# Cross attention's query projection with the tokens' high and low part moving together, and another order of the first loads

## The chip, the cores and the metric

The kernel is one layer of a decoder and runs on one core of a Trainium2 chip. The metric is the time of one execution on the device in microseconds (us), taken as the median of several runs. The engines of the core are named as in the profile: PE is TensorE's matmul and PEld its weight load, DVE is VectorE, ACT is ScalarE, POOL is GpSimd, SP is SyncE, which here only issues transfers.

## The reference

All of it is float32, with 256 tokens of width 1024 (`x`), 256 memory tokens (`mem`) and one layer:

```python
z = h @ w_in[l]                                  # u | q | k | v, 512 columns each
pool_out = multiscale_pool(u, w_pool[l], pool_scale[l])
attn_out = moba_attention(q, k, v)               # 8 heads of 64; at 256 tokens plain causal attention
mix = jnp.concatenate([pool_out, attn_out], axis=-1) @ w_out[l]
h = layer_norm(DEEPNORM_ALPHA * h + mix, ln1_g[l], ln1_b[l])
h = layer_norm(DEEPNORM_ALPHA * h + memory_cross_attention(h, mem, w_xq[l], w_xkv[l], w_xo[l]),
               ln2_g[l], ln2_b[l])
h = layer_norm(DEEPNORM_ALPHA * h + swiglu(h, w_gate[l], w_up[l], w_down[l]), ln3_g[l], ln3_b[l])

def memory_cross_attention(h, mem, w_xq, w_xkv, w_xo):   # 4 heads of 256
    q = (h @ w_xq).reshape(B_, S_, XATTN_HEADS, XATTN_HEAD_DIM)
    kv = mem @ w_xkv
    ...
    s = jnp.einsum('bshd,bmhd->bhsm', q, k, ...) * (XATTN_HEAD_DIM ** -0.5)
    p = jax.nn.softmax(s, axis=-1)
    o = jnp.einsum('bhsm,bmhd->bshd', p.astype(v.dtype), v).reshape(B_, S_, D)
    return o @ w_xo
```

`swiglu` has 2816 hidden columns: `(silu(h @ w_gate) * (h @ w_up)) @ w_down`.

## The kernel before

**Products in three parts.** Each operand of a large product is split into a high part, which is the number rounded to `float32r`, and a low part, which is what is left. A product is then high by high, high by low and low by high, three matmuls that add up in PSUM. `split` does this for activations: ScalarE copies the high part (line 319), VectorE subtracts it (line 320). `split_scaled` (lines 323 and 324) does the same with a factor. `Both` keeps a high and a low part side by side in one tile, so that one matmul can move both, 512 columns wide.

**The stream of weights.** `Stream` (`ws`) holds all weights as numbered tiles in the order of their use: w0 to w14 for queries, keys and values (w0 to w5 are 128 x 512, the next 128 x 1024), then the pooling input, cross attention's keys, the output projection, cross attention's values (w35 to w42), cross attention's queries (`c_xq`, w43 to w50, two tiles of four rows of k for each head), its output projection (w51 to w58), the gate and up weights (`c_gu`, from w59, four tiles for each of eleven chunks) and the down projection. `fetch` issues the transfers, seven raw tiles ahead. `prepare` casts a tile to its high part on ScalarE (line 95) and subtracts it on VectorE into the low part (line 96). There are eight high and eight low buffers, so tile i goes into the place of tile i - 8. `get` hands out a tile, and on the way prepares one more tile if fewer than `used + 8` are prepared; `done` counts `used` up when the last row of a tile has been multiplied. The order of the instructions on every engine is the order in which the code emits them: the schedule is written by hand, with generators that `run` advances by a given number of steps.

**The start.** `keep_busy` gives TensorE matmuls on zeros. The tokens come transposed, in blocks of 128 rows (`load_xt`, line 198): the first on SP's queue, the second on ScalarE's. Tile w0 comes in two halves by `ws.cuts`: the first on ScalarE's queue, the second on SP's. Then w1, w2, w3 and so on follow on SP's queue. `ws.casts` cuts the cast of w0 into three. `product_qk` (line 390) multiplies w0 with the first block of tokens, then w1 with the same block, then w2 and w3 with the second block.

**Cross attention.** `h1T` holds the tokens transposed, as two tiles, one for the high and one for the low part. `do_xq(h)` projects a head's queries with `proj_t` (line 274): for each of eight rows k and each of two halves f three matmuls of 256 columns, into one PSUM bank, then one `split_scaled` for the whole head. It yields 16 times. `xscores(h)` multiplies the queries with the keys (lines 256 to 258; the queries' parts are the stationary operand), takes maximum, exponentials and sum, and scales. `xprobs_t(h)` transposes the probabilities (line 716) and splits them, `xattend(h)` multiplies them with the values. The heads are interleaved by hand: five steps of head h + 1 stand between the projection of head h and its scores, up to head 2. The scores of head 3 come behind three steps of the output projection `project(c_xo, ...)`.

**Feed-forward.** `product_gu` makes a chunk's gate and up products in four PSUM banks: a pass over eight rows with the high weights, each moving both parts of `h2T` (line 804, 512 columns), then a pass with the low weights that moves the high part alone (line 811, 256 columns). In the first of these chunks `gated_t` (line 793) transposes the gated first chunk `sg0` in the middle of the high pass. `Gated.add` (lines 830 and 831) adds the two parts of a chunk.

Of the kernel before, what the change touches and what calls it, by code (L numbers as in the profile page):

```python
# [8 lines left out]
F32 = mybir.dt.float32  # L9
F32R = mybir.dt.float32r  # L10
AF = mybir.ActivationFunctionType
OP = mybir.AluOpType
AX = mybir.AxisListType

P = 128
D = 1024
S = 256
T = S // P
KD = D // P
# [12 lines left out]
RAW_BUFS, W_BUFS, AHEAD = 7, 8, 8  # L32
A8_BUFS = 9
PR_BUFS = 6
# [3 lines left out]
def r32(t):  # L38
    return t.bitcast(F32)


class Stream:
# [40 lines left out]
    def prepare(self, upto, eng=None):  # L83
        nc = self.nc
        while len(self.tiles) < min(upto, len(self.src)):
            i = len(self.tiles)
            src = self.src[i]
            for split in self.splits.pop(i, []):
                split()
            self.fetch(i + 1, nc.sync)  # L90
            raw = self.raws[i]
            hi = self.pool.tile(list(src.shape), F32R, tag="hi", name=f"w{i}h")
            lo = self.pool.tile(list(src.shape), F32R, tag="lo", name=f"w{i}l")
            for s in self.casts.get(i, [slice(None)]):
                nc.scalar.copy(hi[:, :, s], raw[:, :, s])  # L95
            (eng or nc.vector).tensor_sub(lo, raw, r32(hi))
            self.tiles.append((hi, lo))
            self.fetch(max(i + 1, len(self.homes)) + RAW_BUFS, nc.sync)

# [26 lines left out]
def decoder_layer(  # L126
# [3 lines left out]
    nc = tc.nc  # L130
# [3 lines left out]
    sp = ctx.enter_context(tc.tile_pool(name="small", bufs=3))  # L134
# [6 lines left out]
    def a8(name, dt=F32):  # L141
        return ap.tile([P, KD, S], dt, tag="a8", name=name)

    def bank(name):
        return pb.tile([P, 512], F32, tag="b", name=name)
# [5 lines left out]
    ws = Stream(nc, wp)  # L151

    def cols(w, c):

        return ws.add(w[c])
# [4 lines left out]
    def block(w, at, shape):  # L160

        j, n = shape
        return w[at:at + P * j * n].rearrange("(p j n) -> p j n", p=P, j=j)
# [6 lines left out]
        else:  # L170
            c_qk.append(ws.add(block(w_qkv, k * P * 1024, (2, 512)), 1))
    c_v = [ws.add(block(w_qkv, (KD + i) * P * 1024, (2, 512)), 1) for i in range(KD // 2)]
    ws.cuts[0] = [(slice(0, 256), nc.scalar), (slice(256, 512), nc.sync)]
    ws.casts[0] = [slice(0, 128), slice(128, 256), slice(256, 512)]
    c_u = [cols(w_u, c) for c in range(2)]
    c_xk = [cols(w_xk, c) for c in range(4)]
    c_mix = [rows(w_out, k, 0) for k in range(KD)]
# [1 line left out]
    c_xq = [cols(w_xq, c) for c in range(4)]  # L179
    c_xo = [rows(w_xo, k, 0) for k in range(KD)]  # L180
    c_gu = [ws.add(w_gu[c], 4) for c in range(NFC)]
# [10 lines left out]
    xr = a8("xr")  # L192
# [1 line left out]
    ws.homes = [home[0][:, n:n + 1, :] for n in range(4)]  # L194
    ws.homes += [home[1][:, 0:1, :], home[1][:, 1:2, :], home[1][:, 2:4, :]]

    def load_xt(k, n=2, queue=nc.sync):
        queue.dma_start(xr[:, k:k + n, :], block(x_t, k * P * S, (n, S)))

    def split_xt(k, n=2):  # L200
        split(xT[0][:, k:k + n, :], xT[1][:, k:k + n, :], xr[:, k:k + n, :])
# [58 lines left out]
    def pair(hl, *ix):  # L260
        return hl[0][ix], hl[1][ix]
# [3 lines left out]
    def proj_t(pss, numbers, yT):  # L265


        for k in range(KD):
            hi, lo = ws.get(numbers, k)
            y_hi, y_lo = pair(yT, ALL, k)  # L270
            for f in range(2):
                s = slice(f * P, (f + 1) * P)
                for n, (w, y) in enumerate(((hi, y_hi), (hi, y_lo), (lo, y_hi))):
                    nc.tensor.matmul(pss[f], w[:, s], y, start=k == 0 and f == 0 and n == 0,  # L274
                                     stop=k == KD - 1 and n == 2, skip_group_check=True)
                if f == 1:
                    ws.done(numbers, k)
                yield
# [31 lines left out]
    def run(gen, n=None):  # L310

        while n is None or n > 0:
            if next(gen, gen) is gen:
                return False
            n = None if n is None else n - 1
        return True

    def split(h, l, ps):
        nc.scalar.copy(h, ps)  # L319
        nc.vector.tensor_sub(l, ps, r32(h))  # L320

    def split_scaled(h, l, ps, scale):
        nc.scalar.mul(h, ps, scale)  # L323
        nc.vector.scalar_tensor_tensor(l, ps, scale, r32(h), op0=OP.mult, op1=OP.subtract)  # L324
# [18 lines left out]
    def transpose_tok(dst, tok, t, k0):  # L343

        ps = bank("tp")
        for k in range(4):
            nc.tensor.transpose(ps[:, k * P:(k + 1) * P], tok[:, (k0 + k) * P:(k0 + k + 1) * P], ident)  # L347
        ts = slice(t * P, (t + 1) * P)
        h, l = dst.parts(k0, 4, ts) if isinstance(dst, Both) else (d[:, k0:k0 + 4, ts] for d in dst)
        split(h, l, ps.rearrange("p (k t) -> p k t", k=4))  # L350


    qkT = a8("qkT")
# [11 lines left out]
    def keep_qk(i):  # L365

        dst = qkT[:, 2 * i:2 * i + 2, :]
        if i == 0:
            nc.scalar.mul(dst, qk[i], HD ** -0.5)
        elif i == 1:  # L370
            nc.vector.tensor_scalar(dst, qk[i], HD ** -0.5, None, op0=OP.mult)
        elif i == 2:
            nc.scalar.copy(dst, qk[i])
        else:
            nc.vector.tensor_copy(dst, qk[i])

    def product_qk(k):


        x_hi, x_lo = pair(xT, ALL, k)  # L380
        for j in range(2):
            hi, lo = ws.get(c_qk[k], j)
            halves = (2 * j, 2 * j + 1)
            order = [(i, f, hi, y) for i in halves for f in range(2) for y in (x_hi, x_lo)]
            if k == j == 0:
                order = [(i, f, hi, y) for i in halves for y in (x_hi, x_lo) for f in range(2)]
            order += [(i, f, lo, x_hi) for i in halves for f in range(2)]
            for i, f, w, y in order:
                c = 2 * (i % 2) + f
                nc.tensor.matmul(qk[i][:, f, :], w[:, c * P:(c + 1) * P], y,  # L390
                                 start=k == 0 and f == 0 and w is hi and y is x_hi,
                                 stop=k == KD - 1 and w is lo, skip_group_check=True)
                if k == KD - 1 and w is lo and f == 1:
                    keep_qk(i)
            ws.done(c_qk[k], j)
# [2 lines left out]
    for k in range(2, KD, 2):  # L398
        ws.before_split(c_qk[k][0], lambda k=k: split_xt(k))
    load_xt(0, 1)  # L400
    ws.fetch(1, None)
    load_xt(1, 1, nc.scalar)
    ws.fetch(4, nc.sync)
    load_xt(2)
    ws.fetch(7, nc.sync)
    load_xt(4)
# [263 lines left out]
        norm.finish()  # L670
    run(mix)
    ws.held = False
    h1T = (a8("h1Th", F32R), a8("h1Tl", F32R))

    xv = [ap.tile([P, T, D], F32R, tag="a8", name=f"xv{i}") for i in range(2)]

# [16 lines left out]
    oT = (a8("oTh", F32R), a8("oTl", F32R))  # L693
    xqT, xpr, xpt = {}, {}, {}

    def do_xq(h):
        ps = (bank if h == 0 else accbank)("pxq").rearrange("p (f t) -> p f t", f=2)
        yield from proj_t([ps[:, f, :] for f in range(2)], c_xq[h], h1T)
        xqT[h] = [sp.tile([P, 2, S], F32R, name=f"xq{i}", tag="pr", bufs=PR_BUFS) for i in range(2)]
        split_scaled(*xqT[h], ps, 256 ** -0.5)  # L700

    def xscores(h):
        ps = bank("xs").rearrange("p (t s) -> p t s", t=2)
# [25 lines left out]
    xq = [do_xq(h) for h in range(XH)]  # L729
# [3 lines left out]
    run(xq[1])  # L733
    run(xq[2], 5)
    xscores(1)
    run(xq[2], 6)
    xprobs_t(0)
    run(xq[2])
    run(xq[3], 6)
    xscores(2)  # L740
    xattend(0)
    run(xq[3], 6)
    xprobs_t(1)
    run(xq[3])

# [13 lines left out]
    h2T = Both("h2T")  # L759
# [29 lines left out]
    def gated_t():  # L789
        pt = bank("pgt").rearrange("p (f t) -> p f t", f=2)  # L790
        for t in range(T):
            for f in range(2):
                nc.tensor.transpose(pt[:, f, t * P:(t + 1) * P], sg0[:, t, f * P:(f + 1) * P], ident)
        split(gT[0][0][:, 0:2, :], gT[0][1][:, 0:2, :], pt)

    def product_gu(pss, numbers):

        n = ws.src[numbers[0]].shape[1]  # L800
        for k in range(KD):
            hi, _ = ws.get(numbers, k)
            for b, ps in enumerate(pss):
                nc.tensor.matmul(ps, hi[:, b * P:(b + 1) * P], h2T.both(k), start=k == 0, stop=False,  # L804
                                 skip_group_check=True)
            if k % n == n - 1:
                yield
        for k in range(KD):
            _, lo = ws.parts_of(numbers, k)
            for b, ps in enumerate(pss):  # L810
                nc.tensor.matmul(ps[:, S:], lo[:, b * P:(b + 1) * P], h2T.pair(k)[0], start=False,  # L811
                                 stop=k == KD - 1, skip_group_check=True)
            ws.done(numbers, k)
            if k % n == n - 1:
                ws.prepare(min(ws.used + AHEAD, len(ws.tiles) + 1))
                yield

    class Gated:


# [31 lines left out]
    left = None  # L852
    for c in range(1, NFC):
        pss = [(accbank if c % 2 else bank)("pg") for _ in range(4)]
        gu = product_gu(pss, c_gu[c])
        run(gu, 1)
        if left:
            left.multiply()
        run(gu, 1)
        if left:  # L860
            left.split()
        else:
            gated_t()
        run(gu)
        left = Gated(c, pss)
        left.add()
# [37 lines left out]
    left = until(dn)[1]  # L904
# [57 lines left out]
```

## Time and profile before

| | |
|---|---|
| median of 3 runs | 384.67 us (384.36 to 385.12) |
| profiled execution | 384.89 us, span 383.1 us from the first to the last instruction |
| granted TensorE clock, mean | 0.995 |
| TensorE busy | 373.4 us, 97% of the span |
| VectorE, ScalarE, GpSimd busy | 259.7, 187.6 and 19.0 us |
| the chain that ended last | 94% on TensorE |
| transfers | 71.93 MB, mean 188 GB/s |
| stretch of the query projections (131.78 to 163.33 us) | TensorE busy 31.55 us of 31.55, VectorE 21.42, ScalarE 15.72 |

The rows of a timeline begin with start and duration in us, then the engine, the line of the code, the operation, `out<-in` by the program's names and the shapes; in brackets stands how long the engine was idle before it and what ended that. Rows of matmuls can overlap, since they are pipelined: their starts are what counts. A row of the waits names who waited, on whom, and then the total in us, the number of times and the longest. `DMA` in the chain is a transfer, from its issue to its landing.

### The profile page before, as it was taken

The page shows a single profiled execution, that of the slowest core. Times are in us where ns is not written, and L with a number is a line of the kernel's source. Part 1 is how long each engine was busy: PE and PEld are TensorE (multiplying, and loading weights), DVE is VectorE, ACT ScalarE, POOL GpSimd, SP SyncE. Part 2 cuts the span into 40 slices and gives each one's busy share as a digit, 9 for nine tenths or more (in the row PEclk, how much of TensorE's full clock was granted, in tenths as well). Part 3 has the DMA queues.
Part 4 walks back from the last instruction along what each step waited for, and adds up shares of the span by engine and source line. Part 5 has one row for each costly group of instructions (what it writes and reads, how often), then busy time and mean ns, then how long its engine had stood idle before and what let it go on. Part 6 is the DMA issues. An engine that isn't in the chain of part 4 may idle for free.

```text
span 383.1 us, 5778 instructions
## 1 busy us (share of the span) xinstructions
PE 373.4 (97%) x2236; PEld 330.2 (86%) x2236; DVE 259.7 (68%) x390; ACT 187.6 (49%) x293; POOL 19.0 (5%) x31
## 2 busy tenths in 40 slices
PE   8999999999999999999999999999999999999992
PEld 7997989898888899988887888888888888888881
DVE  5758889954699766665888766666776667444275
ACT  5646677544164644454147455566445564334000
POOL 1000036300010000000100000000000000000000
PEclk9999999999999999999999999999999999999998
DMA  8997674668509953433109854456655758630011
GB/s 266 409 413 252 214 285 120 229 193 284 169 1 325 357 196 116 137 134 109 56 0 322 285 174 165 171 204 220 217 187 153 285 178 270 194 110 2 0 46 64
DMA packets 21322, 71.93 MB, mean 188 GB/s; under 512 B 2480, under 2 KB 3504, under 8 KB 21168
## 3 DMA queue, kind: packets, MB, share of 16 engines
q1 hardware_dynamic: 20720, 71.05, 54.2%
q10 hardware_dynamic: 576, 0.52, 0.4%
q8 instruction: 17, 0.28, 0.3%
q14 instruction: 9, 0.07, 0.0%
HBM read 70.52 MB, written 1.05 MB: 187 GB/s over the span
## 4 chain that ended last, share of the span: by engine, by line
PE 94%; ACT 1%; DVE 1%; DMA 1%; issue 1%; SPq 0%; DVEq 0%; ACTq 0%
PE pg L804 18%; PE pg L811 10%; PE acc L256 9%; PE acc L257 9%; PE acc L258 9%; PE pxq L274 6%; PE pxk L274 6%; PE pqk L390 6%; PE pu L274 3%; PE xv L258 2%; PE xv L256 2%; PE xv L257 2%; DMA wr<-in_w_qkv 1%; PE pv L256 1%; PE pv L257 1%; PE pv L258 1%
## 5 line engine op out<-in xcount | busy, mean ns | idle before, releaser
L830 ACT COPY sg<-pg 128x256 f32<-128x256 f32 x40 | 12.0, 387 | 23.5 <-PE pg L811 23.5
L611 POOL TENSOR_TENSOR rs<-rs,mhalf 128x1 f32<-128x1 f32 x6 | 5.0, 832 | 302.5 <-DVE rs L610 302.5
L835 ACT ACTIVATE sg<-sg 128x512 f32<-128x512 f32 x10 | 6.3, 633 | 16.7 <-DVE sg L831 16.7
L831 DVE TENSOR_TENSOR sg<-pg,sg 128x256 f32<-128x256 f32 x40 | 14.1, 414 | 0.0
L600 DVE SCALAR_TENSOR_TENSOR r<-h,acc 128x256 f32<-128x256 f32 (+1 forms) x10 | 5.1, 519 | 10.9 <-PE acc L258 10.9
L320 DVE TENSOR_TENSOR gTl<-sg,gTh 128x512 fp32r<-128x512 f32 x10 | 6.9, 692 | 6.2 <-ACT gTh L319 6.2
L426 ACT ACTIVATE pr<-pr,mx 128x128 f32<-128x128 f32 (+1 forms) x16 | 7.1, 445 | 6.8 <-DVE mx L457 6.8
L319 ACT CAST gTh<-sg 128x512 fp32r<-128x512 f32 x10 | 6.2, 621 | 7.8 <-DVE sg L836 7.8
L426 ACT ACTIVATE xpr<-xs,mx 128x256 f32<-128x256 f32 x8 | 3.7, 470 | 10.2 <-DVE mx L437 10.2
L319 ACT CAST h2T<-tp 128x512 fp32r<-128x512 f32 x4 | 2.4, 588 | 12.9 <-PE tp L347 12.9
L603 DVE BATCH_NORM_STATS2 st<-r 128x6 f32<-128x512 f32 (+1 forms) x14 | 8.1, 580 | 0.5
L836 DVE TENSOR_TENSOR sg<-sg 128x512 f32<-128x512 f32 x10 | 6.9, 693 | 1.4 <-ACT sg L835 0.5
L616 DVE SCALAR_TENSOR_TENSOR r<-r,mv,g 128x512 f32<-128x512 f32 x11 | 7.9, 744 | 0.0
L501 POOL TENSOR_TENSOR win<-win 128x269 f32<-128x269 f32 (+2 forms) x6 | 6.5, 1084 | 0.5
L501 POOL TENSOR_TENSOR win<-upad 128x271 f32<-128x271 f32 x4 | 3.5, 871 | 54.8 <-ACT upad L529 54.8
L431 DVE RECIPROCAL sm<-sm 128x2 f32<-128x2 f32 x12 | 2.0, 166 | 5.9 <-ACT xpr L426 4.5
L622 DVE SCALAR_TENSOR_TENSOR h<-r,rs,b 128x512 f32<-128x512 f32 x8 | 5.7, 747 | 0.2
L319 ACT CAST h1Th<-tp 128x512 fp32r<-128x512 f32 x4 | 2.3, 587 | 7.1 <-PE tp L347 7.1
L323 ACT ACTIVATE xq<-pxq 128x512 fp32r<-128x512 f32 x4 | 2.4, 598 | 5.3 <-PE pxq L274 5.3
L324 DVE SCALAR_TENSOR_TENSOR xq<-pxq,xq 128x512 fp32r<-128x512 f32 x4 | 2.8, 692 | 3.3 <-ACT xq L323 3.3
L457 DVE CUSTOM_DVE_ANT_0 pr<-ps,tri 128x128 f32<-128x128 f32 (+1 forms) x16 | 4.7, 352 | 0.2 <-PE ps L450 0.2
L95 ACT CAST w39h<-w39r 128x1024 fp32r<-128x1024 f32 x1 | 1.1, 1057 | 7.8 <-PE acc L258 7.8
(1018 smaller groups left out, 1374.5 us busy)
## 6 DMA issues: line engine op xcount, KB each, us to landing
g<-in_ln_g SPq DMA_DIRECT2D x3, 512.0 KB, 5.4
b<-in_ln_b SPq DMA_DIRECT2D x3, 512.0 KB, 7.4
wr<-in_w_qkv SPq DMA_DIRECT2D x5, 256.0 KB, 4.9
mr<-in_mem_t SPq DMA_DIRECT2D x1, 1024.0 KB, 12.0
xt<-in_x SPq DMA_DIRECT2D x1, 1024.0 KB, 8.6
xr<-in_x_t SPq DMA_DIRECT2D x3, 256.0 KB, 6.5
wr<-in_w_qkv SPq DMA_DIRECT2D x1, 512.0 KB, 6.4
w7r<-in_w_qkv SPq DMA_DIRECT2D x1, 512.0 KB, 6.6
```

The source lines that it names most:

```text
L256: nc.tensor.matmul(ps, wa, ya, start=start, stop=False, skip_group_check=part)
L257: nc.tensor.matmul(ps, wa, yb, start=False, stop=False, skip_group_check=part)
L258: nc.tensor.matmul(ps, wb, ya, start=False, stop=stop, skip_group_check=part)
L274: nc.tensor.matmul(pss[f], w[:, s], y, start=k == 0 and f == 0 and n == 0, stop=k == KD - 1 and n == 2, skip_group_check=True)
L319: nc.scalar.copy(h, ps)
L390: nc.tensor.matmul(qk[i][:, f, :], w[:, c * P:(c + 1) * P], y, start=k == 0 and f == 0 and w is hi and y is x_hi, stop=k == KD - 1 and w i ...
L426: nc.scalar.activation(dst[:, j, :], src[:, j, :], AF.Exp, bias=mx[:, j:j + 1], scale=sign, accum_out=sm[:, j:j + 1])
L501: nc.gpsimd.tensor_add(nxt[:, 2 * n - 1:], cur[:, 2 * n - 1:], cur[:, n - 1:PADW + S - n])
L804: nc.tensor.matmul(ps, hi[:, b * P:(b + 1) * P], h2T.both(k), start=k == 0, stop=False, skip_group_check=True)
L811: nc.tensor.matmul(ps[:, S:], lo[:, b * P:(b + 1) * P], h2T.pair(k)[0], start=False, stop=k == KD - 1, skip_group_check=True)
L830: nc.scalar.copy(y[:, f, :], ps[:, S:])
L831: nc.vector.tensor_add(y[:, f, :], ps[:, :S], y[:, f, :])
```

## The change

1. `product_gu` becomes `proj_both`, which takes the moving tokens as an argument, works for heads of queries and for chunks, yields after every row k (it did so at the end of a tile), and asks for the next tile's preparation after every row of its low pass, right behind `done`.
2. `h1T` becomes a `Both`. `do_xq` calls `proj_both` with two PSUM banks, one for each half f of a head, high-part products in columns 0 to 255 and products with the low part in columns 256 to 511. The split has three steps for each half: ScalarE scales to the high part, VectorE takes what is left of the first columns (`left`), VectorE adds the scaled second columns to that (`lo`). The steps of head 2 and head 3 between the other work are 5 where they were 6.
3. `gated_t` comes after the whole high pass of its chunk.
4. Both halves of w0 are loaded on ScalarE's queue; w1 follows the first block of tokens on SP's queue, then the second block of tokens. The subtraction of w0 is done in two halves, each behind the casts of its half, and the first tile's matmuls go by halves: high by high, high by low and low by high of the first half, then of the second.

```diff
@@ Stream.prepare
-            for s in self.casts.get(i, [slice(None)]):
-                nc.scalar.copy(hi[:, :, s], raw[:, :, s])
-            (eng or nc.vector).tensor_sub(lo, raw, r32(hi))
+            for group in self.casts.get(i, [[slice(None)]]):
+                for s in group:
+                    nc.scalar.copy(hi[:, :, s], raw[:, :, s])
+                s = slice(group[0].start, group[-1].stop)
+                (eng or nc.vector).tensor_sub(lo[:, :, s], raw[:, :, s], r32(hi[:, :, s]))
@@ the first loads
-    ws.cuts[0] = [(slice(0, 256), nc.scalar), (slice(256, 512), nc.sync)]
-    ws.casts[0] = [slice(0, 128), slice(128, 256), slice(256, 512)]
+    ws.cuts[0] = [(slice(0, 256), nc.scalar), (slice(256, 512), nc.scalar)]
+    ws.casts[0] = [[slice(0, 128), slice(128, 256)], [slice(256, 512)]]
...
+            order += [(i, f, lo, x_hi) for i in halves for f in range(2)]
             if k == j == 0:
-                order = [(i, f, hi, y) for i in halves for y in (x_hi, x_lo) for f in range(2)]
-            order += [(i, f, lo, x_hi) for i in halves for f in range(2)]
+                order = [(i, f, w, y) for i in halves for w, y in ((hi, x_hi), (hi, x_lo), (lo, x_hi))
+                         for f in range(2)]
...
     load_xt(0, 1)
-    ws.fetch(1, None)
-    load_xt(1, 1, nc.scalar)
+    ws.fetch(2, nc.sync)
+    load_xt(1, 1)
     ws.fetch(4, nc.sync)
@@ cross attention
-    h1T = (a8("h1Th", F32R), a8("h1Tl", F32R))
+    h1T = Both("h1T")
...
+    def proj_both(pss, numbers, yT):
+        for k in range(KD):
+            hi, _ = ws.get(numbers, k)
+            for b, ps in enumerate(pss):
+                nc.tensor.matmul(ps, hi[:, b * P:(b + 1) * P], yT.both(k), start=k == 0, stop=False,
+                                 skip_group_check=True)
+            yield
+        for k in range(KD):
+            _, lo = ws.parts_of(numbers, k)
+            for b, ps in enumerate(pss):
+                nc.tensor.matmul(ps[:, S:], lo[:, b * P:(b + 1) * P], yT.pair(k)[0], start=False,
+                                 stop=k == KD - 1, skip_group_check=True)
+            ws.done(numbers, k)
+            if not ws.held:
+                ws.prepare(min(ws.used + AHEAD, len(ws.tiles) + 1))
+            yield
     def do_xq(h):
-        ps = (bank if h == 0 else accbank)("pxq").rearrange("p (f t) -> p f t", f=2)
-        yield from proj_t([ps[:, f, :] for f in range(2)], c_xq[h], h1T)
-        xqT[h] = [sp.tile([P, 2, S], F32R, name=f"xq{i}", tag="pr", bufs=PR_BUFS) for i in range(2)]
-        split_scaled(*xqT[h], ps, 256 ** -0.5)
+        pss = [(bank if h == 0 else accbank)("pxq") for _ in range(2)]
+        yield from proj_both(pss, c_xq[h], h1T)
+        xqT[h] = hi, lo = [sp.tile([P, 2, S], F32R, name=f"xq{i}", tag="pr", bufs=PR_BUFS) for i in range(2)]
+        left = sp.tile([P, 2, S], F32, name="xql", tag="pr", bufs=PR_BUFS)
+        for f, ps in enumerate(pss):
+            nc.scalar.mul(hi[:, f], ps[:, :S], 256 ** -0.5)
+            nc.vector.scalar_tensor_tensor(left[:, f], ps[:, :S], 256 ** -0.5, r32(hi[:, f]),
+                                           op0=OP.mult, op1=OP.subtract)
+            nc.vector.scalar_tensor_tensor(lo[:, f], ps[:, S:], 256 ** -0.5, left[:, f],
+                                           op0=OP.mult, op1=OP.add)
@@ the heads' interleaving
-    run(xq[2], 6)
+    run(xq[2], 5)
     xprobs_t(0)
     run(xq[2])
-    run(xq[3], 6)
+    run(xq[3], 5)
     xscores(2)
     xattend(0)
-    run(xq[3], 6)
+    run(xq[3], 5)
     xprobs_t(1)
     run(xq[3])
@@ the feed-forward chunks
-        gu = product_gu(pss, c_gu[c])
-        run(gu, 1)
+        gu = proj_both(pss, c_gu[c], h2T)
+        run(gu, 2)
         if left:
             left.multiply()
-        run(gu, 1)
+        run(gu, 2)
         if left:
             left.split()
         else:
+            run(gu, 4)
             gated_t()
         run(gu)
```

More of the change, by code (lines that the diff above doesn't have):

```diff
@@ L195, in decoder_layer, with load_xt @@
     ws.homes += [home[1][:, 0:1, :], home[1][:, 1:2, :], home[1][:, 2:4, :]]
-    def load_xt(k, n=2, queue=nc.sync):
-        queue.dma_start(xr[:, k:k + n, :], block(x_t, k * P * S, (n, S)))
+    def load_xt(k, n=2):
+        nc.sync.dma_start(xr[:, k:k + n, :], block(x_t, k * P * S, (n, S)))
     def split_xt(k, n=2):
@@ L348, in transpose_tok @@
         ts = slice(t * P, (t + 1) * P)
-        h, l = dst.parts(k0, 4, ts) if isinstance(dst, Both) else (d[:, k0:k0 + 4, ts] for d in dst)
-        split(h, l, ps.rearrange("p (k t) -> p k t", k=4))
+        split(*dst.parts(k0, 4, ts), ps.rearrange("p (k t) -> p k t", k=4))
     qkT = a8("qkT")
@@ L794, in gated_t @@
         split(gT[0][0][:, 0:2, :], gT[0][1][:, 0:2, :], pt)
[L796 to L816, printed above, removed]
     class Gated:
```

## The prediction

> **What bounds the kernel now.** I read the page first (its busy times), then TensorE's waits, then the chain that ended last, and last the timelines of TensorE, VectorE and ScalarE around the three places that the change touches.
>
> ```profile
> PE 373.4 (97%) x2236; PEld 330.2 (86%) x2236; DVE 259.7 (68%) x390; ACT 187.6 (49%) x293; POOL 19.0 (5%) x31
> PE pqk L390 <- ACT w1h L95: 0.9, 1, 0.9
> PE busy L361 <- PEq L926: 0.8, 1, 0.8
> PE pgt L793 <- DVE sg L787: 0.6, 1, 0.6
> ```
>
> TensorE is busy for 97% of the span, and the last three lines are all of its waits. So a microsecond taken from its stream, or from one of those waits, shortens the kernel; and a wait that is put into its stream anywhere lengthens it, since nothing later stands idle to absorb it. These are the chain's pieces for the projection and for the feed-forward products:
>
> ```profile
> 140.93 5.76 PE pxq L274 x48
> 215.53 7.28 PE pg L804 x32
> 222.81 3.83 PE pg L811 x32
> ```
>
> 48 matmuls over 256 columns take 5.76 us, 0.120 each; 32 over 512 columns 7.28 us, 0.2275 each; 32 over 256 again 0.120 each. That prices the new form: L804 and L811 already do what the queries will do.
>
> **Part 1, fewer matmuls for the queries.** A head had 8 x 2 x 3 = 48 matmuls of 256 columns. It gets 16 of 512 (both parts of the tokens) and 16 of 256. Each of the 16 pairs becomes one: 2 x 0.120 - 0.2275 = 0.0125 us less. Four heads: 64 x 0.0125 = **-0.80 us**, all on the path. The Trainium skill (TensorE: Matmul & The Clock Gate, Back-to-back issue gap) puts a warm matmul at N/2.4 ns plus a fixed 2.5 ns, by which 64 fewer matmuls would give an estimated 0.16 us. The trace does not agree with that fixed part (0.120 us is 13 ns over 256/2.4), and by the page the sum below would be 0.64 us higher.
>
> **Part 2, what the new low-part pass queues ahead of the query split.** This is the term that decides. Before, a tile's `done` was answered by the next `get`, that is, by head h+1 and behind the split of head h. In `proj_both` the low pass calls `prepare` itself, after rows 3 and 7 of a head. So two weight tiles (w51 and w52 for head 0) are now cast and subtracted ahead of the split on ScalarE's and VectorE's in-order queues. Their low halves go into the slots of the tiles eight earlier (w43, w44), which are read until the end of rows 3 and 7 of the low pass. The feed-forward stage shows this:
>
> ```profile
> 223.60 1.12 PE L811 MATMUL pg<-h2T,w68l 128*128 128x256 f32 x8
> 223.85 1.23 DVE L96 TENSOR_TENSOR w75l<-w75r,w75h 128x1024 fp32r<-128x1024 f32 x1 [2.98 <-PE pg L811]
> 225.00 1.22 DVE L96 TENSOR_TENSOR w76l<-w76r,w76h 128x1024 fp32r<-128x1024 f32 x1
> 226.13 1.22 DVE L96 TENSOR_TENSOR w77l<-w77r,w77h 128x1024 fp32r<-128x1024 f32 x1
> 228.40 1.41 DVE L831 TENSOR_TENSOR sg<-pg,sg 128x256 f32<-128x256 f32 x4
> 226.32 1.20 ACT L830 COPY sg<-pg 128x256 f32<-128x256 f32 x4 [2.38 <-PE pg L811]
> ```
>
> VectorE stands still 2.98 us until TensorE has left w67l (when w68l begins, plus the matmul's latency), then works off the subtractions 1.14 us apart, and the adds that wait for the same products come behind. Nobody waits there. After a query projection somebody does: the scores, ten matmuls later. Now the same queue in the query stage before:
>
> ```profile
> 131.78 0.28 PE L274 MATMUL pxq<-h1Th,w43h 128*128 128x256 f32 x1
> 137.73 0.60 ACT L323 ACTIVATE xq<-pxq 128x512 fp32r<-128x512 f32 x1 [1.95 <-PE pxq L274]
> 138.36 0.69 DVE L324 SCALAR_TENSOR_TENSOR xq<-pxq,xq 128x512 fp32r<-128x512 f32 x1 [1.32 <-ACT xq L323]
> 139.29 1.23 DVE L96 TENSOR_TENSOR w52l<-w52r,w52h 128x1024 fp32r<-128x1024 f32 x1 [0.24 <-ACT w52h L95]
> 140.65 0.28 PE L258 MATMUL xs<-xkTh,xq 128*128 128x256 f32 x1
> 140.97 0.69 DVE L437 TENSOR_REDUCE mx<-xs 128x2 f32<-128x512 f32 x1 [0.45 <-PE xs L258]
> 143.69 1.23 DVE L96 TENSOR_TENSOR w53l<-w53r,w53h 128x1024 fp32r<-128x1024 f32 x1
> 150.77 0.59 ACT L319 CAST xst<-xpt 128x512 fp32r<-128x512 f32 x1
> ```
>
> The split is finished at 139.05 and the first matmul that needs its low part is the third score: it starts at 139.57, so 0.5 us of slack. The new split is longer too: for each of the two halves a scaling on ScalarE and two dependent VectorE operations (`left`, then `lo`). I price each at 0.41 us like the adds of L831 (1.41 us for four: 0.34 apart), the dependent one 0.45 after its input; ScalarE's scaling at a copy of L830, hidden under the subtractions. A walk through the queues, TensorE first and then VectorE:
>
> Head 0: first matmul 131.78, high pass 3.64, low pass 1.92, ten matmuls of head 1 2.275: scores at 139.61. VectorE: w51l from 136.59 (when row 3 of the low pass is through), w52l 137.73 (1.14 later; row 7 was through at 137.50), `left` 138.87, `lo` 139.33, the second half's 139.67 and 140.13, usable at 140.60. The sixth score needs that at 140.21: 0.39 late.
>
> Head 1, counted from the start of the last score before: the maximum starts at +0.32 (140.65, 140.97), and 2.72 later (143.69) VectorE is free for weights. Two subtractions (2.28) and the split (0.45 + 0.34 + 0.45 + 0.42 + 0.05) end at +7.03. TensorE is at its sixth score after 0.12 + 1.365 + 1.92 + 2.275 + 0.6 = +6.28. 0.75 late.
>
> Head 2: the same, with four transposes (0.44) for TensorE and the probabilities' split on VectorE between. The transposes are issued from +1.97, ScalarE's cast of that split (0.59) runs from +2.58 to +3.17, so its subtraction stands at +3.22, w55l waits for its own cast until +4.17, and the second half of the split is usable at +8.16. TensorE needs it at +6.72. 1.44 late.
>
> Head 3's scores come after 4 us of other work, but the output projection takes up the two PSUM banks that its split reads: 0.3 us late.
>
> A stall in front of a weight load costs more than the wait. The start shows it:
>
> ```profile
> 6.88 0.39 PE L390 MATMUL pqk<-xTh,w1h 128*128 128x256 f32 x1 [0.88 <-ACT w1h L95]
> 7.11 0.28 PE L390 MATMUL pqk<-xTl,w1h 128*128 128x256 f32 x1
> 7.22 0.28 PE L390 MATMUL pqk<-xTh,w1h 128*128 128x256 f32 x1
> ```
>
> The stalled matmul keeps the engine 0.23 us instead of 0.12; I add 0.11 for each head of 0 to 2. Stalls: 0.50 + 0.86 + 1.55 + 0.3 = **+3.2 us**. The same walk with the old code puts no wait anywhere and ends the stage where the trace does (within 0.05 us). Bounds: with the VectorE operations of the split right behind each other (0.34) 2.4; with gaps twice as long 3.8.
>
> **Part 3, `gated_t` four rows later.** Its transposes now come after 32 matmuls instead of 16.
>
> ```profile
> 196.97 0.60 PE L347 MATMUL tp<-ident,h 128*128 128x128 f32 x4
> 197.32 0.48 PE L256 MATMUL pg<-w59h,h2T 128*128 128x512 f32 x1
> 206.60 0.38 PE L793 MATMUL pgt<-ident,sg 128*128 128x128 f32 x2
> 207.59 0.44 PE L793 MATMUL pgt<-ident,sg 128*128 128x128 f32 x2 [0.61 <-DVE sg L787]
> 207.78 2.09 PE L804 MATMUL pg<-h2T,w65h 128*128 128x512 f32 x8
> 207.12 0.41 DVE L787 TENSOR_TENSOR sg<-sg,pg 128x256 f32<-128x256 f32 x1
> 212.74 1.23 DVE L96 TENSOR_TENSOR w71l<-w71r,w71h 128x1024 fp32r<-128x1024 f32 x1 [3.36 <-PE pg L811]
> ```
>
> Four transposes that wait for nothing hold TensorE 0.35 us (196.97 to 197.32); these hold it 1.18 (206.60 to 207.78). `sg` is there at 207.53 and will be asked for near 210.2 (206.60 and 16 x 0.2275), so **-0.8 us** (0.6 to 0.85). The split that moves along falls into VectorE's 3.36 us of idleness before w71l.
>
> **Part 4, first loads.** Tile 0's second half goes from SP's to ScalarE's queue, the tokens' second block the other way, behind w1; w1 is issued one place earlier.
>
> ```profile
> 4.51 0.69 DVE L96 TENSOR_TENSOR w0l<-wr,w0h 128x512 fp32r<-128x512 f32 x1 [0.60 <-ACT w0h L95]
> 5.26 0.74 PE L390 MATMUL pqk<-xTh,w0l 128*128 128x256 f32 x4
> 1.65 4.55 DMA wr<-in_w_qkv
> 1.18 0.45 ACTq L198 DMA_DIRECT2D xr<-in_x_t  x1
> xr<-in_x_t ACTq DMA_DIRECT2D x1, 128.0 KB, 3.1
> 3.06 0.43 SPq L198 DMA_DIRECT2D xr<-in_x_t  x1
> xr<-in_x_t SPq DMA_DIRECT2D x1, 256.0 KB, 5.2
> 8.30 0.19 PEld L390 LDWEIGHTS pqk<-xTh,w2h 128*128 128x128 f32 x1
> ```
>
> TensorE runs out of tile 0 at 5.74 and waits for w1, issued at 1.65 and landed at 6.20. One place earlier is an issue 0.47 us sooner, with 128 KB less in front. The 256 KB of tokens issued at 3.06, three loads of 256 KB behind w1, landed at 8.26, 2.06 us after it, which is 0.69 us for 256 KB and 0.34 for 128. I take **-0.4 us**. Bounds: 0 if w1 only shares the engines with tile 0's second half; 1.2 if TensorE waits for nothing more, since with the halved subtraction it is done with tile 0 near 5.5. The tokens' second block, now behind w1, lands no later than w1 did (6.2); its split takes 0.4 and is wanted when w2 starts, 7.9 instead of 8.30. Halving tile 0's subtraction alone is worth nothing while w1 lands last. The finer `run` steps of the feed-forward loop leave its order as it was.
>
> **The sum.** -0.8 + 3.2 - 0.8 - 0.4 = +1.2 us on the profiled execution, whose span of 383.1 us went with 384.89 us; the median of the three runs is 384.67, so **385.9 us**, 0.3% slower.
>
> **The rivals.** *Faster: the subtractions do not hold up the split.* If VectorE gets w51l and w52l (and their successors) done before the head's last matmul, the split starts when it did, the scores find it 0.1 us early, and the stage is 0.8 us shorter: 384.67 - 0.8 - 0.8 - 0.4 = 382.7. It decides at 0.6 to 0.75 us: by so much VectorE's way must be shorter than walked in heads 1 and 2. For it: VectorE is idle a third of the time. Against it: the 2.98 us row, in which it is idle because the slot is not free. Chance 0.25. *The start gives all it can.* w1 lands before 4.9, TensorE goes on at 5.5: 1.2 instead of 0.4, 385.1. For it: the tokens' second block, next in line before, landed at 4.28, nearly 2 us ahead of w1, so something other than bytes held w1 up, and an earlier w1 may slip past it. Chance 0.12. *The start gives nothing and the bank wait doubles*: 386.6. Chance 0.08. *The wider matmul saves nothing* can be left out: L804 is the same instruction.
>
> **The numbers.** The forecast as walked has 0.55; the bounds of the stalls and of the start give it a range of its own of 384.3 to 386.9. 0.2% (0.77 us) is about what a measurement of this kernel can tell from no change, as the three runs lie 0.76 apart. Of the forecast's 0.55, 0.44 is slower by more and 0.11 within (short stalls, a good start). The fast rival gives 0.23 faster and, if the stalls go only in part, 0.02 within; the good start 0.09 within and 0.03 slower; the bad start 0.08 slower. Together 0.23 faster, 0.22 the same, 0.55 slower. The range reaches down into the fast rival to where a third of its lead is gone, 383.3, and up to 386.9.
>
> **What would show it.** In the profile after: TensorE's waits gain lines for the scores with VectorE's `lo` as releaser, about 0.4, 0.75 and 1.4 us, and lose `pgt`; in VectorE's timeline w52l starts only when TensorE leaves w44l, with `left` behind it; a head's 32 matmuls take 5.56 us; w1's cast begins near 5.8. No wait at the scores would prove part 2, and the sign, wrong; w1's cast before 5.2 would show the second rival.

## The result and the profile after

The changed kernel takes 385.73 us (median of 15 runs, 385.55 to 386.43), the kernel before in the same comparison 385.04 us (15 runs, 383.80 to 385.48). The ratio is 1.0025, with a 95% interval of 1.0017 to 1.0033: about 1.0 us slower (0.65 to 1.27). The ratio is one of means, which lie 0.95 us apart; the two medians lie 0.69 apart. The forecast was 385.9, 1.2 us slower.

The profiled execution took 385.97 us, its span is 384.2 us. From the page of the profile after, and all of TensorE's waits (who waited on whom, total, times, longest):

```profile
PE 374.3 (97%) x2172; PEld 327.6 (85%) x2172; DVE 263.3 (69%) x403; ACT 187.8 (49%) x297; POOL 19.0 (5%) x31
PE xs L260 <- DVE xq L728: 1.4, 4, 0.9
PE busy L362 <- PEq L934: 0.8, 1, 0.8
```

64 matmuls fewer, and TensorE is busy for longer. The waits for w1 and for the gated rows are gone; in their place stand four at the scores, all released by line 728, the `lo` of the new split. The total of 1.4 us understates them. The record of the matmul before is 0.28 us long where starts are 0.12 apart, so it covers 0.16 us of each wait, and the stalled matmul's own record is 0.11 us longer (0.39). What a wait costs is read from starts. TensorE's timeline after: the first score of heads 0, 1 and 2 and the first instruction behind each set of twelve, for head 2 also its two stalled scores, then the first product of the output projection and the first score of head 3:

```profile
138.83 0.28 PE L258 MATMUL xs<-xkTh,xq 128*128 128x256 f32 x1
140.76 1.55 PE L705 MATMUL pxq<-h1T,w46h 128*128 128x512 f32 x6
146.36 0.28 PE L258 MATMUL xs<-xkTh,xq 128*128 128x256 f32 x1
148.60 1.09 PE L705 MATMUL pxq<-h1T,w48h 128*128 128x512 f32 x4
154.62 0.28 PE L258 MATMUL xs<-xkTh,xq 128*128 128x256 f32 x1
155.88 0.39 PE L260 MATMUL xs<-xkTh,xq 128*128 128x256 f32 x1 [0.86 <-DVE xq L728]
156.67 0.38 PE L260 MATMUL xs<-xkTh,xq 128*128 128x256 f32 x1 [0.17 <-DVE xq L728]
157.60 0.28 PE L258 MATMUL xo<-xst,xv 128*128 128x256 f32 x1
164.68 0.48 PE L258 MATMUL acc<-w51h,oTh 128*128 128x512 f32 x1
169.34 0.28 PE L258 MATMUL xs<-xkTh,xq 128*128 128x256 f32 x1
```

Twelve scores without a wait take 1.44 us. These took 1.93, 2.24 and 2.98: 0.49, 0.80 and 1.54 us lost, where the walk had 0.50, 0.86 and 1.55. The eighteen products took 4.66 us; before they took 4.20 (163.33 to 167.53), so 0.46 was lost at the banks, for 0.3 walked. Together 3.3 us (3.2 walked). The walk had one stall in each head, at the sixth score. In heads 1 and 2 the trace has two, since the third score already waits for the first half's `lo` (155.88) and the sixth for the second half's (156.67); the sums agree all the same, because VectorE's last `lo` sets when the sixth score can start. VectorE's timeline after shows the queue behind it:

```profile
135.83 1.23 DVE L98 TENSOR_TENSOR w51l<-w51r,w51h 128x1024 fp32r<-128x1024 f32 x1 [1.07 <-issue]
136.97 1.22 DVE L98 TENSOR_TENSOR w52l<-w52r,w52h 128x1024 fp32r<-128x1024 f32 x1
138.11 0.42 DVE L726 SCALAR_TENSOR_TENSOR xql<-pxq,xq 128x256 f32<-128x256 f32 x1
138.56 0.42 DVE L728 SCALAR_TENSOR_TENSOR xq<-pxq,xql 128x256 fp32r<-128x256 f32 x1
138.90 0.41 DVE L726 SCALAR_TENSOR_TENSOR xql<-pxq,xq 128x256 f32<-128x256 f32 x1
139.35 0.42 DVE L728 SCALAR_TENSOR_TENSOR xq<-pxq,xql 128x256 fp32r<-128x256 f32 x1
```

w51l and w52l first, then the four operations of the split, 0.45 and 0.34 us apart. The walk had them 0.76 to 0.78 us later on its own clock (138.87 for the first), which is the 0.78 us that the whole stage starts earlier.

Four starts divide TensorE's stream into parts that can be compared: the first query matmul, the first matmul of w52 behind `xattend(2)` (`acc<-w52h`), the first of w63 and the first of w67 (from there to the start of TensorE's last matmul it is 160.0 us in both). Before, then after; the first query matmul before (131.78) and the rows of `pgt` stand in the prediction:

```profile
170.40 0.40 PE L256 MATMUL acc<-w52h,oTh 128*128 128x512 f32 x1
202.97 1.98 PE L804 MATMUL pg<-h2T,w63h 128*128 128x512 f32 x8
215.36 2.00 PE L804 MATMUL pg<-h2T,w67h 128*128 128x512 f32 x8
```

```profile
131.00 1.98 PE L705 MATMUL pxq<-h1T,w43h 128*128 128x512 f32 x8
172.21 0.40 PE L258 MATMUL acc<-w52h,oTh 128*128 128x512 f32 x1
204.91 1.98 PE L705 MATMUL pg<-h2T,w63h 128*128 128x512 f32 x8
212.17 0.60 PE L822 MATMUL pgt<-ident,sg 128*128 128x128 f32 x4
212.53 1.20 PE L711 MATMUL pg<-h2T,w63l 128*128 128x256 f32 x8
216.44 0.86 PE L705 MATMUL pg<-h2T,w67h 128*128 128x512 f32 x3
```

| part | before | after | difference | forecast |
|---|---|---|---|---|
| to the first query matmul | 131.78 | 131.00 | -0.78 | -0.4 |
| cross attention, to `acc<-w52h` | 38.62 | 41.21 | +2.59 | +2.4 |
| to w63 | 32.57 | 32.70 | +0.13 | 0 |
| to w67, with `pgt` | 12.39 | 11.53 | -0.86 | -0.8 |
| sum | | | +1.08 | +1.2 |

The transposes of `pgt` stand in one row without a wait and hold TensorE 0.36 us (212.17 to 212.53).

### The profile page after: what moved, and what is told of

Read it like the earlier page. It is cut to its first block, busy times and chain, and to the rows that moved or that the text cites. A ratio compares the mean times of both kernels' runs of the same rounds, so it can differ in the third digit from the quotient of the medians.

```text
span 384.2 us, 5668 instructions
## 1 busy us (share of the span) xinstructions
PE 374.3 (97%) x2172; PEld 327.6 (85%) x2172; DVE 263.3 (69%) x403; ACT 187.8 (49%) x297; POOL 19.0 (5%) x31
## 4 chain that ended last, share of the span: by engine, by line
PE 93%; DVE 4%; issue 1%; ACT 1%; DVEq 0%
PE pg L705 19%; PE pg L711 10%; PE acc L258 9%; PE acc L259 9%; PE acc L260 9%; PE pqk L392 6%; PE pxk L276 6%; PE pu L276 3%; PE xv L260 2%; PE xv L259 2%; PE xv L258 2%; PE pxq L705 2%; PE pv L258 1%; PE pg L260 1%; PE tp L349 1%
## 5 line engine op out<-in xcount | busy, mean ns | idle before, releaser
L260 PE MATMUL xs<-xkTh,xq 128*128 128x256 f32 x16 | 5.1, 320 | 1.5 <-DVE xq L728 1.4
L321 ACT CAST h1T<-tp 128x512 fp32r<-128x512 f32 x4 | 2.4, 588 | 7.1 <-PE tp L349 7.1
L439 DVE TENSOR_REDUCE mx<-xs 128x2 f32<-128x512 f32 x4 | 2.8, 692 | 4.1 <-PE xs L260 4.1
L260 PEld LDWEIGHTS xs<-xkTh,xq 128*128 128x128 f32 x16 | 3.0, 188 | 2.5 <-DVE xq L728 2.5
L349 PEld LDWEIGHTS tp<-ident,h 128*128 128x128 f32 x32 | 3.9, 141 | 1.3 <-PE pg L260 0.4
```

What stands on the lines that cost most here:

```text
L260: nc.tensor.matmul(ps, wb, ya, start=False, stop=stop, skip_group_check=part)
```

## Experiments

Theory: the two weight preparations that the new low pass puts ahead of the split make the scores late. Rival: the split itself, four dependent operations for one, does. All times below are medians, with the ratio to the kernel before in the same comparison (384.60 us in the first four, 384.85 in the rest).

**The change, preparation left to the next `get`.**

```diff
-            if not ws.held:
+            if yT is not h1T:
                 ws.prepare(min(ws.used + AHEAD, len(ws.tiles) + 1))
```

> The change, with one line less: the low pass of a query head does not ask for a tile's preparation, so the next head's get does, behind the split. Queue theory (the two weight subtractions ahead of the split make the scores late): all waits at the scores and at the output projection's banks go, the stage of cross attention from the first query matmul to the output projection's seventh comes out 0.8 us shorter than in the kernel before (after: 2.6 longer), and the time is 3.3 us under the changed kernel, near 382.5 us. Rival (the split itself, four dependent VectorE operations instead of one, makes the scores late): at least half of the 3.3 us of waits stays, 384 us or more.

Measured: 382.54 us, ratio 0.9952 (0.9940 to 0.9965). TensorE's one wait left is the one at the very start. VectorE's timeline of this run:

```profile
137.09 0.42 DVE L726 SCALAR_TENSOR_TENSOR xql<-pxq,xq 128x256 f32<-128x256 f32 x1 [2.27 <-ACT xq L725]
137.55 0.42 DVE L728 SCALAR_TENSOR_TENSOR xq<-pxq,xql 128x256 fp32r<-128x256 f32 x1
137.89 0.41 DVE L726 SCALAR_TENSOR_TENSOR xql<-pxq,xq 128x256 f32<-128x256 f32 x1
138.34 0.42 DVE L728 SCALAR_TENSOR_TENSOR xq<-pxq,xql 128x256 fp32r<-128x256 f32 x1
138.68 1.22 DVE L98 TENSOR_TENSOR w51l<-w51r,w51h 128x1024 fp32r<-128x1024 f32 x1
```

and TensorE's, the ends of the stage:

```profile
131.05 1.52 PE L705 MATMUL pxq<-h1T,w43h 128*128 128x512 f32 x6
168.94 0.40 PE L258 MATMUL acc<-w52h,oTh 128*128 128x512 f32 x1
```

VectorE waits 2.27 us for the split's input with nothing ahead, does the same four operations, and then the subtraction. The stage lasts 37.89 us, 0.73 less than before. So the split's length by itself costs nothing: the rival falls. By its ratio this version is 1.8 us faster than the kernel before, and by the two ratios some 2.8 us faster than the changed kernel; the spans of the profiled executions are 380.9, 383.1 and 384.2 us.

**The query part alone on the kernel before** (`proj_both`, `Both`, the split in halves, 5 steps for 6).

> The kernel before with the query part of the change alone (proj_both, split in halves, steps 5 for 6); first loads and gated_t as before. Queue theory: 2.5 us slower than before, 387.5 us, with waits at the scores of 0.5, 0.8 and 1.5 us. If the slowdown comes from the loads or from the moved transposes: within 0.8 us of before.

Measured: 387.49 us, ratio 1.0079 (1.0067 to 1.0092). Its stage lasts 41.19 us (131.62 to 172.81), as in the changed kernel. The slowdown is all there; the other two edits give back.

**Only the preparation after row 7 left to the next `get`.**

```diff
-            if not ws.held:
+            if yT is not h1T or k < KD - 1:
                 ws.prepare(min(ws.used + AHEAD, len(ws.tiles) + 1))
```

> The change, with only the preparation after a head's last row (row 7) left to the next get; the one after row 3 stays ahead of the split. Queue theory: VectorE has one subtraction (1.14 us) less ahead of each split, so heads 0 and 1 wait for nothing and head 2 about 0.4 us: 383.0 us, 2.8 under the changed kernel. If any preparation ahead of the split costs its share, half of the gain of leaving both: 384.1 us. Rival (the split itself): as the changed kernel, 385.7 us.

Measured: 382.90 us, ratio 0.9964 (0.9950 to 0.9978). Heads 0 and 1 wait for nothing, head 2 does. Its scores' sixth matmul and the subtraction that is still ahead, in the timelines of this run:

```profile
153.76 0.28 PE L259 MATMUL xs<-xkTl,xq 128*128 128x256 f32 x1
154.20 0.39 PE L260 MATMUL xs<-xkTh,xq 128*128 128x256 f32 x1 [0.16 <-DVE xq L728]
154.42 0.28 PE L258 MATMUL xs<-xkTh,xq 128*128 128x256 f32 x1
```

```profile
151.33 1.23 DVE L98 TENSOR_TENSOR w55l<-w55r,w55h 128x1024 fp32r<-128x1024 f32 x1 [0.25 <-ACT w55h L96]
```

It starts 0.32 us late (154.20 for 153.88) and keeps TensorE 0.22 us instead of 0.12: 0.42 us, as expected. A preparation ahead costs nothing until the slack is used up; what goes beyond the slack counts in full. The cost is a threshold, no share of each.

**The old projection and the old split, with the preparation ahead of it.** (`early` is a new argument of `proj_t`, true for the heads of queries.)

```diff
                 if f == 1:
                     ws.done(numbers, k)
+                    if early:
+                        ws.prepare(min(ws.used + AHEAD, len(ws.tiles) + 1))
```

> The kernel before, old projection and old split, but a head's projection asks for the next preparation right behind done, ahead of the split. Queue theory: the cast and the subtraction of one tile, both waiting for the tile's last matmul, stand ahead of the split: waits at the scores of about 1.1, 1.1 and 0.8 us, 3 us slower than before, 388 us. Rival (the new split's length is what costs): no slower than before.

Measured: 388.02 us, ratio 1.0093 (1.0079 to 1.0107). ScalarE's and VectorE's rows and the third score of head 0:

```profile
137.62 1.05 ACT L95 CAST w52h<-w52r 128x1024 fp32r<-128x1024 f32 x1 [1.83 <-PE pxq L274]
138.57 0.59 ACT L325 ACTIVATE xq<-pxq 128x512 fp32r<-128x512 f32 x1
139.84 0.68 DVE L326 SCALAR_TENSOR_TENSOR xq<-pxq,xq 128x512 fp32r<-128x512 f32 x1
139.46 0.28 PE L257 MATMUL xs<-xkTl,xq 128*128 128x256 f32 x1
140.58 0.39 PE L258 MATMUL xs<-xkTh,xq 128*128 128x256 f32 x1 [0.84 <-DVE xq L326]
```

With none of the new matmuls and none of the new split the scores come late by 1.0 us, and the stage lasts 41.65 us (131.79 to 173.44). Here ScalarE's cast waits for the projection's end as well, since the old order reads the high weights to the end. So the order makes a loss without the new code, here on two engines; with the run that defers the preparation, the cause is shown from both sides.

**The new start alone.** (Loads, and tile 0 by halves.)

> The kernel before with the new start alone (order of the loads, and tile 0's subtraction and matmuls by halves). By the prediction's estimate 0.4 us faster than before; by the trace of the changed kernel, in which w2's first matmul starts at 7.63 instead of 8.42, 0.8 us faster: 384.2 us.

Measured: 383.96 us, ratio 0.9978 (0.9969 to 0.9987): 0.85 us faster.

**The new order of the loads alone.**

> The kernel before with the new order of the loads alone; tile 0 is subtracted in one piece and multiplied in the old order. If an earlier w1 is the whole gain: w1's cast begins before 5.0 us instead of 6.2 and w1's first matmul follows tile 0's last without a wait, 0.6 to 0.8 us faster than before. If the halves are needed: 0.3 us or less.

Measured: 384.52 us, ratio 0.9998 (0.9986 to 1.0010). No gain that the ratio tells, though w1's cast begins at 4.80. (The median is 0.33 us lower; one of the eleven executions took 386.54.)

**Tile 0's halves alone.**

> The kernel before with tile 0's halves alone (subtraction and matmuls), loads as before. w1 lands at 6.2 us as before and ends the wait, so within 0.1 us of before. If the halves matter by themselves: 0.3 us or more faster.

Measured: 384.91 us, ratio 1.0001 (0.9991 to 1.0010). The start of three timelines: tile 0's matmuls and the first on w1, casts on ScalarE. First the loads alone, then the halves alone, then the changed kernel:

```profile
4.38 0.63 PE L390 MATMUL pqk<-xTl,w0h 128*128 128x256 f32 x2
4.95 0.80 PE L390 MATMUL pqk<-xTh,w0h 128*128 128x256 f32 x2
5.54 0.63 PE L390 MATMUL pqk<-xTl,w0h 128*128 128x256 f32 x2
5.96 0.87 PE L390 MATMUL pqk<-xTh,w0l 128*128 128x256 f32 x4
6.67 0.28 PE L390 MATMUL pqk<-xTh,w1h 128*128 128x256 f32 x1
4.80 0.61 ACT L95 CAST w1h<-wr 128x512 fp32r<-128x512 f32 x1
```

```profile
5.29 0.40 PE L393 MATMUL pqk<-xTh,w0l 128*128 128x256 f32 x2
6.94 0.39 PE L393 MATMUL pqk<-xTh,w1h 128*128 128x256 f32 x1 [1.25 <-ACT w1h L96]
6.27 0.62 ACT L96 CAST w1h<-wr 128x512 fp32r<-128x512 f32 x1 [1.94 <-DMA wr<-in_w_qkv]
```

```profile
4.49 0.41 ACT L96 CAST w0h<-wr 128x256 fp32r<-128x256 f32 x1 [0.52 <-DMA wr<-in_w_qkv]
4.80 0.61 ACT L96 CAST w1h<-wr 128x512 fp32r<-128x512 f32 x1
4.85 0.63 PE L392 MATMUL pqk<-xTh,w0l 128*128 128x256 f32 x2
5.28 0.62 PE L392 MATMUL pqk<-xTh,w0h 128*128 128x256 f32 x2
6.20 0.28 PE L392 MATMUL pqk<-xTh,w1h 128*128 128x256 f32 x1
```

With the halves alone TensorE is done with tile 0 near 5.5 and waits 1.25 us for w1. With the loads alone w1 is no longer the limit: its cast begins at 4.80, while tile 0's matmuls last until 6.67. Between the first half's high part and the second half (4.95) TensorE has nothing to do for about 0.15 us; in the changed kernel the low part of the first half (4.85) fills that time, and w1 is ready behind. The rest of the difference between 6.67 and 6.20 can't be put down to the order of tile 0: in the profile of the loads alone the matmuls still come 0.21 us apart from 5.54 to 5.96 instead of 0.12, while in the changed kernel's that slow pace ends at 5.7 (the last section comes back to it). So the times show that neither alone is worth what both are, and the traces show w1 as the limit as long as the loads are the old ones. How much the halves add behind the new loads, and by what, is not shown by these single profiles.

**`gated_t` alone.**

> The kernel before with gated_t behind the whole high pass of its chunk, nothing else. TensorE's wait for the gated rows goes: 0.8 us faster than before, 384.2 us. If something behind the moved split gets late: less than 0.4 us.

Measured: 383.93 us, ratio 0.9974 (0.9965 to 0.9984): 0.6 to 1.3 us faster. Its stretch from w63 (202.28) to w67 (213.80) lasts 11.52 us instead of 12.39.

## Why the prediction was right, and where its sizes were off

The three edits timed alone add up to what they do together: +3.0 (1.0079), -0.85 and -1.0 (0.9974) make +1.2 us, measured +1.0. The forecast of +1.2 comes closer than its terms do: in the profiles part 4 brings 0.38 us more than forecast and part 3 0.06, while the stage of cross attention costs 0.19 more and the stretch behind it 0.13, so that the sum is off by only 0.12. That the misses cancel is luck; that part 2 outweighs the gains is not.

- **Part 1, the wider matmuls:** forecast -0.80, measured -0.73 (the stage of the deferring run). The price from the feed-forward products carried over. The 0.16 us by the Trainium skill's gap (TensorE: Matmul & The Clock Gate, Back-to-back issue gap) does not agree with this; the section itself calls that gap the isolated one, and says that in a stream with weight loads both instructions set the spacing.
- **Part 2, the queue:** forecast +3.2, measured +3.3, head by head within 0.06 us, at the banks 0.46 for 0.3. The deferring run and the early one show it as the cause.
- **Part 3, `gated_t`:** forecast -0.8, measured -0.86.
- **Part 4, the first loads:** forecast -0.4, measured -0.78 in the trace and -0.85 in time. This is the term that was mis-sized. The step that failed is w1's landing: I took 128 KB less in front as 0.34 us and put w1's cast near 5.8; it began at 4.80, and there it stood behind ScalarE's cast of w0's second half (4.49), since w1 had landed at 4.3. In the five profiles with w1 second on SP's queue w1 landed 3.1 to 3.3 us after its issue at 1.18, in the five with w1 third 3.9 to 4.6 after 1.65. The second rival had named this ("something other than bytes held w1 up"), and its landing "before 4.9" came true; what held w1 up stays open. Its price of 1.2 was not reached in the times (0.85): TensorE then had tile 0 itself to finish, until 6.2 in the changed kernel's profile and 5.85 in that of the new start alone, instead of the 5.5 assumed. A single pair of profiles does not give this price: w2's first matmul comes 0.79 us earlier than before in the one (7.63 for 8.42) and 1.13 in the other (7.29), since the slow pace of the first matmuls ends at different times (last section) and w1's landing in the old order varies by 0.7 us itself. That halving tile 0 alone "is worth nothing while w1 lands last" held; that the loads alone would show so little was not seen.
- Not in the sum: 0.13 us between cross attention and w63. One of VectorE's scalings there (line 624) starts 0.46 us after the operation before it instead of 0.11, and the transposes of its rows come 0.2 us later, in the changed kernel and its two variants with all three edits, and in no run with one edit. The profile names no other engine for that wait. Why is open; no run was made for it.

The fast rival (the subtractions do not hold up the split) put the time without that queue at 382.7; the deferring run has 382.54. The rival priced another kernel rightly, one line away; its condition, that VectorE gets the subtractions done in time, did not hold (w52l starts at 136.97, when TensorE is already at w45, since 136.53).

## What to carry to other kernels

When a loop is reused for another consumer, look at what it emits besides its products: a helper that prepares the next tile is harmless behind a product nobody waits for, and costs whatever exceeds the slack when it stands ahead of an eviction that the next matmuls need. Walk the queue from the last matmul to the first reader: here two subtractions ahead cost 3.3 us, one cost 0.42 and none cost nothing. And time two edits at a start-up together as well as singly: here neither alone showed a gain, and both together 0.85 us.

## What the runs showed of the hardware

- A matmul that stalls for its stationary operand costs 0.10 to 0.11 us more than the wait. That was read from one row before, and held in the stalls at the scores in these runs: its record is 0.38 or 0.39 us instead of 0.28, and the next start comes 0.22 or 0.23 us later instead of 0.12.
- The first matmuls run at little more than half their later pace, for a time that differs from run to run. In the changed kernel's profile they come 0.21 us apart until 5.7 us (4.85 to 5.28 for two); in the run with the new start alone 0.12 from about 4.3 on:

```profile
5.61 0.40 PE L393 MATMUL pqk<-xTh,w0l 128*128 128x256 f32 x2
5.85 0.28 PE L393 MATMUL pqk<-xTh,w1h 128*128 128x256 f32 x1
```

The granted clock reads 1.00 in both stretches, but only because the trace's record of the clock begins later: its entry for full speed starts 5.74 us after the first instruction in the changed kernel's profile, 4.26 in that of the new start alone, 4.12 in that of the kernel before and 6.48 in that of the loads alone. The entry lasts 375.466 us in six of the ten profiles and 372.053 in four, which are 110 and 109 times their difference of 3.413 us; so in these profiles both changes of the clock fall on a grid of that step, and the grid does not begin with the kernel. The Trainium skill (TensorE: Matmul & The Clock Gate, Part 1: The HAM clock gate) states a half-rate clock until a free-running window of some 3.4 us has been busy. The trace agrees: the first pitch is that of half its 2.4 GHz (256 columns in 0.213 us), and the step and the varying moment are those of such a window. The first matmul on w1 comes at 5.85 in the one profile and at 6.20 in the other, so single profiles of the start must not be compared more closely than that.
